# Storing half of the gate weights and all merge weights one superblock later, with x's root row by way of DRAM, cross-attention sums in one matmul, and a rank for readers of the dense banks

## The chip, the cores and the metric

The kernel runs on one core of one Trainium2 chip. The metric is the device time of one execution in microseconds (us). Before the change the median of three runs is 2143.12 us (2143.11 to 2143.8).

In the profile PE is the matmul engine and PEld its weight loads, DVE the vector engine, ACT the scalar engine, POOL GpSimd, and SP the queue that issues most DMAs.

## The reference

One decoder layer over x (2048 tokens x 1024, float32). `h = RMSNorm(x)` is multiplied by one wide matrix `w_in`; its columns feed three branches and their gates.

```
h = rms_norm(x, norm_g);  p = h @ w_in            # 59 blocks of 128 columns
y_a = rwkv7_mix(...)   * silu(z_a)                # delta-rule recurrence, 8 heads x 64
y_b = sliding_window_sink_attn(...) * silu(z_b)   # window 128, 8 query heads x 64
y_c = memory_cross_attn(q, mem ...) * silu(z_c)   # 4 heads x 128, 256 memory tokens
gates = sigmoid(p_gate)                           # 3 x 1024 columns
merged = gates0*(y_a @ w_proj_a) + gates1*(y_b @ w_proj_b) + gates2*(y_c @ w_proj_c)
out = x + merged @ w_out
```

In the cross attention each query head is divided by the root of its mean square over 128 channels; h divides x by such a root over 1024 channels.

## The kernel before

The 2048 tokens are worked off in four superblocks (`sb` 0 to 3) of 512 tokens. Activations lie with channels on the partitions, 512 tokens along a row.

**Dense products.** Float32 accuracy comes from three matmuls in a reduced format (float32r): every operand is split into a high part and the rest, and `gemm3` issues high x high (L534), high x low (L535) and low x high (L536). `proj` (one column block of `w_in`) is 8 such triples into one of two PSUM banks named `mm`; `gate` is a `proj` followed by a tanh on ACT (L1302), `merge` adds 4 triples with a block of `w_proj` and takes the product up on DVE (L1314 or L1317). The 24 column blocks from `B_G` on are those of the gates. `output` multiplies the merged rows by `w_out` (L1334 to L1336). `shift` reads an `mm` bank three times: ACT L739, DVE L740 and, last, DVE L742 (`carry`).

**Weights.** `wblock` fetches half a column block: a raw block of 256 KB (L514) is split by ACT (L515) and DVE (L516) into `whl`, 512 KB. One of the uses also stores the split pair to DRAM (L520), and later uses only load the pair (L511). `keep_at(key)` says at which use a block is stored: 0 for nearly all, 1 for odd blocks of `w_out` and for odd output blocks of branch 0's merge. A block is used once in each superblock. `whl` has 7 buffers, `raw` 3.

**Two streams and a planner.** In a superblock `stream_r` (the recurrence: `rwkv_prep`, `rwkv_inverse`, `rwkv_chain`) and `stream_f` (`cross_head`, `swa_kv`, four `swa_pair` beside the merge of branch 2, the merge of branch 1, the gates of branch 0) are woven together, and `x_sums` adds up the squares of the next superblock's x beside them. The order written that way only gives ranks: `steps` and `lay_out` play the whole program through with assumed durations, on each engine take the ready instruction of lowest rank, and fix that order on PE, DVE, ACT, POOL and SP. Splits and loads of weights get a rank 1000 lower, and an instruction that is not PE's and reads a PSUM bank gets 600 lower.

**The places that the change touches.** `cross_head` sums q*q over the partitions with `spread_sums`: ACT copies the square's high part (L557), DVE makes the rest (L558), and two matmuls with a matrix of ones add them up (L559, L560); this is so in superblocks 1 to 3. `x_scales` turns the sums of `x_sums` into roots on POOL (`rpow`), and `bcast_T` spreads them: a DVE copy (L572), four PE transposes (L574), an ACT copy (L1371) into `rb`. `x_cols` multiplies the next x by `rb` (L1383) and splits it into `hH` and `hL`. `rwkv_chain` fetches its operands chunk by chunk (`big<-fq`, L941, and `big<-fb`, L944); `put` (L758) has stored them.

Of the kernel before, what the change touches and what calls it, by code (L numbers as in the profile page):

```python
# [9 lines left out]
F32 = mybir.dt.float32  # L10
# [5 lines left out]
ALU = mybir.AluOpType  # L16
# [131 lines left out]
def steps(instructions, manual, groups, follow, ahead=1000):  # L148

    out, masks, seen, byname, opener = [], {}, {}, {}, {}  # L150
    for ins in instructions:
        if isinstance(ins, mybir.BassTilePoolBoundary):
            continue
        s = Step(ins, masks)
        for rs, w in ((s.reads, False), (s.writes, True)):
            for name, parts, words, _, psum, _ in rs:
                s.before |= {q for q, w2, p2, m2 in seen.get(name, ()) if (w or w2 or psum) and q is not s and p2 & parts and m2 & words}
        for name, parts, words, *_ in s.reads:
            seen.setdefault(name, []).append((s, False, parts, words))
        for name, parts, words, *_ in s.writes:  # L160
            old = seen.setdefault(name, [])
            old[:] = [x for x in old if x[0] is s or x[2] & ~parts or x[3] & ~words] + [(s, True, parts, words)]
        s.before |= {byname[x] for x in manual.get(ins.name, ())}
        s.before |= {opener.setdefault(r[0], s) for r in s.writes + s.reads} - {s}
        for b in s.before:
            b.after.append(s)
        byname[ins.name] = s
        s.rank = len(out)
        if any(r[0].startswith(("whl", "raw")) and (s.bytes or r[5] == F32R) for r in s.writes):
            s.rank = max(s.rank - ahead, min(s.rank, FRONT))  # L170
        if s.eng != "PE" and any(r[4] for r in s.reads):
            s.rank -= 600
        if s.eng == "DVE" and s.writes and s.writes[0][0].startswith(("ibc", "Yi")):
            s.rank += 500
        out.append(s)
    for a, b in follow.items():
        byname[a].next = byname[b]
    for names in groups:
        group = [byname[n] for n in names]
        group[0].group = group[1:]  # L180
        needs = set().union(*(s.before for s in group)) - set(group)
        for s in group:
            for b in needs - s.before:
                b.after.append(s)
            s.before |= needs
    return out
# [132 lines left out]
def build(tc, A, nsb=4):  # L319
# [19 lines left out]
    def g2(dt=F32, shape=(128, TB)):  # L339
        return gp_.tile(list(shape), dt, name="g2")  # L340
# [155 lines left out]

    def keep_at(key):

        return key[2] % 2 if key[0] == "out" or key[:2] == ("proj", 0) else 0

    def two_parts(raw):

# [52 lines left out]
    def spread_sums(out, w, sq, hi, lo):  # L555

        S.activation(hi, sq, AF.Copy)  # L557
        V.tensor_tensor(lo, sq, hi.bitcast(F32), op=ALU.subtract)  # L558
        PE.matmul(out, w, hi, start=True, stop=False)  # L559
        PE.matmul(out, w, lo, start=False, stop=True)  # L560
# [509 lines left out]
    def cross_head(h, sb, hT, yh, yl):  # L1070
        kv = rp.tile([128, 4, M], F32R, name="km", bufs=2)
        km = kv[:, :2]
        nc.sync.dma_start(km.bitcast(F32), Kd[h // 2][:, :, h % 2])
        if sb:
            vm = kv[:, 2:].rearrange("p u (k c) -> p u k c", k=2)
            nc.sync.dma_start(vm.bitcast(F32), Vs[:, :, :, h * 128:(h + 1) * 128])
        else:
            vm = kv[:, 2].bitcast(F32).rearrange("p (k c) -> p k c", k=2)
            nc.sync.dma_start(vm, Vd[:, :, h * 128:(h + 1) * 128])
        o = proj(B_XQ + h, hT)  # L1080
        qh, ql = g2(F32R), g2(F32R)
        S.activation(qh, o, AF.Copy)
        V.tensor_tensor(ql, o, qh.bitcast(F32), op=ALU.subtract)
        sq = g2()
        S.activation(sq, o, AF.Square)
        yield 1.717
        st = s_ps()
        rs = xp.tile([128, 8], F32, name="st8", bufs=2)
        if sb >= FIRST:
            spread_sums(st, onesw, sq, *(g2(F32R), g2(F32R)))  # L1090
            for i in range(4):
                tk = slice(i * 128, (i + 1) * 128)
                V.tensor_tensor_reduce(sq[:, tk], st[:, tk], ident, 1.0, 0.0, ALU.mult, ALU.add, rs[:, i:i + 1])  # L1093
        else:
            tok_stat(sq, 1, 4, st)
            V.tensor_copy(rs[:, :4], st[:, :4])
        rpow(rs[:, :4], rs[:, :4], 128 * EPS)
        mx = xp.tile([128, 8], F32, name="mx", bufs=2)
        sps = []
        for t2 in range(2):  # L1100
            sp = s_ps().rearrange("p (a m) -> p a m", a=2)
            for i in range(2):
                tk = slice((2 * t2 + i) * 128, (2 * t2 + i + 1) * 128)
                gemm3(sp[:, i], [((qh[:, tk], ql[:, tk]), (km[:, 0], km[:, 1]))])
            V.tensor_reduce(mx[:, 2 * t2:2 * t2 + 2], sp, axis=AX.X, op=ALU.max)
            sps.append(sp)
        V.scalar_tensor_tensor(mx[:, :4], mx[:, :4], -1.0, rs[:, :4], op0=ALU.mult, op1=ALU.mult)
        prs = []
        for t2 in range(2):
            pr = g2(shape=(128, 2, M))  # L1110
            for i in range(2):
                q = 2 * t2 + i
                S.activation(pr[:, i], sps[t2][:, i], AF.Exp, scale=rs[:, q:q + 1], bias=mx[:, q:q + 1],
                             accum_out=mx[:, 4 + q:5 + q])
            prs.append(pr)
        dn = xp.tile([128, 8], F32, name="dn", bufs=2)
        V.tensor_scalar(dn[:, :4], mx[:, 4:], 2.0, None, op0=ALU.mult)
        V.reciprocal(dn[:, :4], dn[:, :4])
        yield 5.667
        if not sb:  # L1120
            oo = o_ps()
            for t2 in range(2):
                pt = s_ps().rearrange("p (k i t) -> p k i t", k=2, i=2)
                for i in range(2):
                    q = 2 * t2 + i
                    scaled_by(prs[t2][:, i], dn[:, q:q + 1], sb)
                    for kt in range(2):
                        PE.transpose(pt[:, kt, i], prs[t2][:, i, kt * 128:(kt + 1) * 128], ident)
                pts = g2(shape=(128, 2, 256))
                S.activation(pts.rearrange("p k t -> p (k t)"), pt.rearrange("p k i t -> p (k i t)"), AF.Copy)  # L1130
                for kt in range(2):
                    PE.matmul(oo[:, t2 * 256:(t2 + 1) * 256], vm[:, kt], pts[:, kt], start=kt == 0, stop=kt == 1)
        else:
            for q in range(4):
                scaled_by(prs[q // 2][:, q % 2], dn[:, q:q + 1], sb)
            pts = []
            for kt in range(2):
                pt = s_ps()
                for q in range(4):
                    PE.transpose(pt[:, q * 128:(q + 1) * 128], prs[q // 2][:, q % 2, kt * 128:(kt + 1) * 128], ident)  # L1140
                pts.append((g2(F32R), g2(F32R)))
                S.activation(pts[kt][0], pt, AF.Copy)
                V.tensor_tensor(pts[kt][1], pt, pts[kt][0].bitcast(F32), op=ALU.subtract)
            oo = o_ps()
            gemm3(oo, [((vm[:, 0, kt], vm[:, 1, kt]), pts[kt]) for kt in range(2)])
        yield 3
        z = silu2(B_ZC + h, hT, gp_.tile([128, TB], F32, name="gt", bufs=2))
        V.tensor_tensor(z, oo, z, op=ALU.mult)
        split_y(z, yh, yl, "c", h, sb)
        yield 6.427  # L1150
# [209 lines left out]
    def x_scales(sb, ss=None):  # L1360

        if not sb:
            rs = row_sums(x0)
        else:
            rs = xp.tile([128, 4], F32, name="rs", bufs=2)
            V.tensor_tensor(rs, ss[:, :, 0], ss[:, :, 1], op=ALU.add)
        rpow(rs, rs, EPS, 1.0 / D)
        bc = s_ps()
        bcast_T(bc, rs, 1, 4)
        rb = tmp()  # L1370
        S.activation(rb, bc, AF.Copy)  # L1371
        return rb
# [23 lines left out]
    for sb in range(nsb):  # L1396
# [41 lines left out]
        gates = []  # L1438
        ss = xp.tile([128, 4, 2], F32, name="ss", bufs=2)
        streams = [paced(g, PACE[min(sb, 1)][i]) for i, g in enumerate((stream_r(), stream_f()))]  # L1440
        if sb + 1 < nsb:
            streams.append(x_sums(sb + 1, ss))
        for _ in weave(*streams):
            pass
        for p in range(4):
# [1 line left out]
        rb = None  # L1447
        if sb + 1 < nsb:
            rope_tables(sb + 1)
            rb = x_scales(sb + 1, ss)  # L1450
        parts = []
        for o in range(8):
            for _ in merge(0, *ya, accs, hT, gates=gates, orange=(o,)):
# [96 lines left out]
```

## Time and profile before

| | |
|---|---|
| profiled execution, its own time | 2143.2 us |
| its span | 2141.4 us |
| TensorE clock granted | 1.0 |
| PE busy | 2125.9 us, 14260 instructions |
| DVE busy | 1418.5 us |
| ACT busy | 802.1 us |
| DMA engines, superblock 0 (540 us) | mostly 0.7 to 1.0 of their time |
| dense triples L534, L535, L536 on `hH`/`hL` | 1888 of each |
| weight stores `k<-whl` | 162 of 512 KB |
| weight reloads `whl<-k` | 474 of 512 KB |

A busy PE is counted from modelled ends: one 128x512 matmul is given some 390 ns, while the next one starts sooner. So the time that one takes from the stream is read from the starts of neighbours, not from its duration. The 1.8 us between the execution's time and the span lie outside of the instructions.

### The profile page before, as it was taken

Reading aid. Unit: us, or ns where it says so; the run is one execution under the profiler, and the core shown is the slowest. Engines: PE = TensorE matmul, PEld = TensorE weight load, DVE = VectorE, ACT = ScalarE, POOL = GpSimd, SP = SyncE. Lnnn points to the kernel's source line nnn. Section 1 sums busy time; section 2 is a strip of 40 time slices with the busy share of each in tenths; the row PEclk is TensorE's granted clock in tenths of the full one; section 3 lists DMA queues with packets and bytes.
Section 4 is the critical chain, followed back from the end, with each engine's and each line's share of the span. In section 5 each row is a group of like instructions: output and inputs, shape, how many; then the busy total and the mean of one; then the engine's idle time right before and its main releaser. Section 6 shows DMA issues by size and latency. Waiting matters only on the chain.

```text
span 2141.4 us, 37426 instructions
## 1 busy us (share of the span) xinstructions
PE 2125.9 (99%) x14260; PEld 1753.8 (82%) x14260; DVE 1418.5 (66%) x3234; ACT 802.1 (37%) x1699; POOL 133.6 (6%) x180
## 2 busy tenths in 40 slices
PE   9999999999999999999999999999999999999999
PEld 7888887778888888878888888887888888888787
DVE  7879888468576787546647778736455777873532
ACT  7655554326344353303424434420423334331220
POOL 1001000001001000001000000000100010000000
PEclk9999999999999999999999999999999999999999
DMA  9988888987866678695876667777676676768665
GB/s 331 364 282 271 272 289 283 340 294 251 285 203 205 192 218 239 198 311 193 281 254 211 201 180 228 236 231 260 216 264 220 197 204 199 233 186 269 217 206 181
DMA packets 308594, 519.17 MB, mean 242 GB/s; under 512 B 89280, under 2 KB 175552, under 8 KB 308416
## 3 DMA queue, kind: packets, MB, share of 16 engines
q1 hardware_dynamic: 292288, 487.42, 70.9%
q10 hardware_dynamic: 16128, 29.37, 4.2%
q8 instruction: 113, 1.85, 0.4%
q14 instruction: 65, 0.53, 0.1%
HBM read 378.80 MB, written 137.89 MB: 241 GB/s over the span
## 4 chain that ended last, share of the span: by engine, by line
PE 91%; DVE 4%; DMA 3%; ACT 1%; issue 1%; POOL 0%; SPq 0%; ACTq 0%; DVEq 0%; POOLq 0%
PE mm L534 23%; PE mm L535 23%; PE mm L536 23%; PE mm L1334 1%; PE mm L1336 1%; PE mm L1335 1%; DMA raw<-in_w_in 1%; PE rw L1016 1%; PE rw L999 1%; PE oo L1283 1%; DVE whl L516 1%; PE rw L831 1%; PE rw L850 1%; DMA k<-whl 1%; PE oo L831 1%
## 5 line engine op out<-in xcount | busy, mean ns | idle before, releaser
L534 PE MATMUL mm<-hH,whl 128*128 128x512 f32 x1888 | 745.2, 395 | 2.0 <-DVE carry L742 1.4
L535 PE MATMUL mm<-hL,whl 128*128 128x512 f32 x1888 | 743.5, 394 | 0.0
L536 PE MATMUL mm<-hH,whl 128*128 128x512 f32 x1888 | 742.5, 393 | 0.0
L534 PEld LDWEIGHTS mm<-hH,whl 128*128 128x128 f32 x1888 | 354.8, 188 | 74.4 <-ACT whl L515 1.8
L536 PEld LDWEIGHTS mm<-hH,whl 128*128 128x128 f32 x1888 | 354.7, 188 | 71.4
L535 PEld LDWEIGHTS mm<-hL,whl 128*128 128x128 f32 x1888 | 355.0, 188 | 70.1 <-DVE hL L1386 0.2
L515 ACT ACTIVATE whl<-raw 128x512 fp32r<-128x512 f32 x174 | 109.1, 630 | 186.4 <-PE mm L536 131.7
L516 DVE TENSOR_TENSOR whl<-raw,whl 128x512 fp32r<-128x512 f32 x174 | 119.2, 687 | 61.7 <-ACT whl L515 55.7
L534 PE MATMUL mm<-yh,whl 128*128 128x512 f32 x384 | 151.4, 394 | 1.3 <-DVE gt L1317 1.2
L535 PE MATMUL mm<-yl,whl 128*128 128x512 f32 x384 | 150.3, 391 | 0.0
L536 PE MATMUL mm<-yh,whl 128*128 128x512 f32 x384 | 149.7, 390 | 0.0
L1302 ACT ACTIVATE gt<-mm 128x512 f32<-128x512 f32 x64 | 37.8, 590 | 179.3 <-PE mm L536 179.0
L534 PEld LDWEIGHTS mm<-yh,whl 128*128 128x128 f32 x384 | 72.1, 188 | 17.2 <-DVE gt L1317 1.6
L1317 DVE SCALAR_TENSOR_TENSOR gt<-gt,mm 128x512 f32<-128x512 f32 x32 | 21.9, 686 | 95.5 <-PE mm L536 95.3
L535 PEld LDWEIGHTS mm<-yl,whl 128*128 128x128 f32 x384 | 72.1, 188 | 15.0 <-DVE yl L1065 0.5
L536 PEld LDWEIGHTS mm<-yh,whl 128*128 128x128 f32 x384 | 72.1, 188 | 14.7
L487 POOL TENSOR_SCALAR st<-st 128x4 f32<-128x4 f32 (+1 forms) x32 | 12.7, 397 | 1019.7 <-DVE st L1093 418.8
L1341 DVE SCALAR_TENSOR_TENSOR ya<-mm,ya 128x512 f32<-128x512 f32 x16 | 11.0, 689 | 93.8 <-PE mm L1336 93.8
L1251 ACT ACTIVATE g<-g,mxs,st 128x128 f32<-128x128 f32 x128 | 61.6, 484 | 28.1 <-DVE mxs L1244 28.1
L892 DVE TENSOR_TENSOR ibc<-km,Yi 128x126 f32<-128x126 f32 (+22 forms) x248 | 62.9, 254 | 7.7 <-DMA km<-fn 2.1
L893 DVE TENSOR_TENSOR Yi<-Yi,ibc 128x126 f32<-128x126 f32 (+22 forms) x248 | 62.7, 253 | 5.6
L491 POOL TENSOR_TENSOR st<-st,mhalf 128x8 f32<-128x8 f32 (+1 forms) x36 | 52.7, 1463 | 3.0
(1828 smaller groups left out, 3579.5 us busy)
## 6 DMA issues: line engine op xcount, KB each, us to landing
whl<-k SPq DMA_DIRECT2D x474, 512.0 KB, 4.2
k<-whl SPq DMA_DIRECT2D x162, 512.0 KB, 4.8
raw<-in_w_in SPq DMA_DIRECT2D x118, 256.0 KB, 4.2
fq<-big SPq DMA_DIRECT2D x64, 256.0 KB, 4.4
fb<-big SPq DMA_DIRECT2D x64, 256.0 KB, 4.3
big<-fq SPq DMA_DIRECT2D x32, 512.0 KB, 6.4
big<-fb SPq DMA_DIRECT2D x32, 512.0 KB, 5.6
ya<-in_x ACTq DMA_DIRECT2D x32, 256.0 KB, 4.7
```

What stands on the lines that cost most here:

```text
L491: G.tensor_tensor(out, out, mhalf[:, :n], op=ALU.pow)
L515: S.activation(w[:, 0], raw, AF.Copy)
L516: V.tensor_tensor(w[:, 1], raw, w[:, 0].bitcast(F32), op=ALU.subtract)
L534: PE.matmul(out, lh, rh, start=i == 0, stop=False)
L535: PE.matmul(out, lh, rl, start=False, stop=False)
L536: newest[0] = PE.matmul(out, ll, rh, start=False, stop=i == n - 1).ins.name
L831: m = PE.matmul(g[:, c], BK[h, c0 + c], Q[h, c0 + c], start=True, stop=True)
L892: V.tensor_tensor(bc[:, :m, :w], Nb[:, s, s + 1:].unsqueeze(1).to_broadcast([128, m, w]), B[:, :m, s:s + 1].to_broadcast([128, m, w]), op= ...
L893: V.tensor_tensor(B[:, :m, s + 1:], B[:, :m, s + 1:], bc[:, :m, :w], op=ALU.add)
L1251: S.activation(P_, P_, AF.Exp, scale=r2[:, b, i:i + 1], bias=mx[:, b, i:i + 1], accum_out=mx[:, b, 2 + i:3 + i])
L1302: S.activation(t, gp, AF.Tanh, scale=0.5)
L1317: V.scalar_tensor_tensor(g, g, 1.0, pp, op0=ALU.add, op1=ALU.mult)
```

## The change

- `keep_at` now also says 1 for odd halves of the gates' column blocks (24) and odd output blocks of the merges of branches 1 and 2 (8): these 32 half blocks are stored in superblock 1 instead of 0, and so are fetched raw and split there once more.
- In `cross_head`, superblocks 1 to 3, DVE first adds the lower 64 rows of the squares to the upper 64; the high part (ACT) and the rest (DVE) of the 64 sums lie one below the other in one tile, and one matmul adds up all 128 rows.
- `x_scales` now runs as a part of the third stream, behind `x_sums`; for superblocks 1 to 3 its roots are stored as a row of 512 numbers in DRAM, and one DMA loads that row into all 128 partitions of `rb`.
- Readers of an `mm` bank get a rank 1600 lower instead of 600.

```diff
         if s.eng != "PE" and any(r[4] for r in s.reads):
-            s.rank -= 600
+            s.rank -= 600 + 1000 * any(r[0].startswith("mm_") for r in s.reads)
...
     def keep_at(key):
-        return key[2] % 2 if key[0] == "out" or key[:2] == ("proj", 0) else 0
+        return key[2] % 2 if key[0] in ("out", "proj") or key[0] == "in" and key[1] >= B_G else 0
...
         if sb >= FIRST:
-            spread_sums(st, onesw, sq, *(g2(F32R), g2(F32R)))
+            half = g2(F32R)
+            V.tensor_tensor(sq[EV], sq[EV], sq[OD], op=ALU.add)
+            S.activation(half[EV], sq[EV], AF.Copy)
+            V.tensor_tensor(half[OD], sq[EV], half[EV].bitcast(F32), op=ALU.subtract)
+            PE.matmul(st, onesw, half, start=True, stop=True)
...
         rpow(rs, rs, EPS, 1.0 / D)
+        if sb:
+            row = dp.tile([1, TB], F32, name=f"xr{sb}")
+            nc.sync.dma_start(row[0].rearrange("(i t) -> t i", t=128), rs)
+            return row
         bc = s_ps()
         bcast_T(bc, rs, 1, 4)
...
+        rows = []
+
+        def stream_x():
+            yield from x_sums(sb + 1, ss)
+            rows.append(x_scales(sb + 1, ss))
+
         if sb + 1 < nsb:
-            streams.append(x_sums(sb + 1, ss))
+            streams.append(stream_x())
...
             rope_tables(sb + 1)
-            rb = x_scales(sb + 1, ss)
+            rb = tmp()
+            nc.sync.dma_start(rb, rows[0].to_broadcast([128, TB]))
```

Since the planner runs anew, the order moves on every engine. Three places in superblock 0 follow. In the changed kernel the lines behind L1087 stand 4 further down (L1275 is the old L1271, L1306 the old L1302), those behind L1371 by 8, and the numbers in tile names differ.

DVE, at the fourth `rwkv_prep`: `mm_3002` is the bank with that head pair's k, `rw`, `oo` and `yps` are banks with its small products, `as_` banks of the window attention. Before:

```order
L839 TENSOR_TENSOR big_2203<-oo_2653,gmask_179 64x512
L839 TENSOR_TENSOR big_2202<-yps_2652,gmask_179 64x512
L516 TENSOR_TENSOR whl_3320<-raw_3321,whl_3320 128x512
L740 SCALAR_TENSOR_TENSOR rk__3041<-mm_3002,c_pv_105,rk__3041 128x511
L1271 TENSOR_TENSOR g2_3121<-as__3114,over_181 64x256
L742 COPY carry1_215<-mm_3002 128x1
```

The same place on DVE in the changed kernel, where the bank is `mm_2990`:

```order
L839 TENSOR_TENSOR big_2202<-yps_2646,gmask_179 64x512
L516 TENSOR_TENSOR whl_3308<-raw_3309,whl_3308 128x512
L1275 TENSOR_TENSOR g2_3109<-as__3102,over_181 64x256
L1275 TENSOR_TENSOR g2_3121<-as__3114,over_181 64x256
L821 SCALAR_TENSOR_TENSOR rr__2521<-rr__2521,dv_182,rk__2245 128x512
L516 TENSOR_TENSOR whl_3450<-raw_3451,whl_3450 128x512
L846 TENSOR_TENSOR big_2205<-big_2205,Pl_658 128x1024
L740 SCALAR_TENSOR_TENSOR rk__3029<-mm_2990,c_pv_105,rk__3029 128x511
L1297 TENSOR_TENSOR g2_3228<-yps_3125,g2_3228 128x512
L742 COPY carry1_215<-mm_2990 128x1
```

Between the last product of the small banks and the last reader of the dense bank (L742) stand eight instructions now instead of three: L821, which lets the next k have its buffer, has moved behind them. On PE the banded product (L1283, now L1287) and eight transposes (L850) have moved in front of the dense block that takes over this bank.

SP, just before `rwkv_chain` begins: `fb` and `fq` are the stored operands of the chain. Before:

```order
L758 DMA fb0_1_654<-big_3000 128x4x128
L514 DMA raw_5350<-in_w_in 128x512
L520 DMA k114_5223<-whl_5218 128x1024
L514 DMA raw_5397<-in_w_in 128x512
L520 DMA k115_5230<-whl_5225 128x1024
L944 DMA big_4254<-fb0_0_653 128x1024
L941 DMA big_4262<-fq0_0_651 128x1024
```

The same place on SP in the changed kernel:

```order
L758 DMA fb0_1_654<-big_2988 128x4x128
L514 DMA raw_5347<-in_w_in 128x512
L514 DMA raw_5354<-in_w_in 128x512
L944 DMA big_4230<-fb0_0_653 128x1024
L941 DMA big_4238<-fq0_0_651 128x1024
```

The two weight stores between the last `put` and the chain's first fetch of `fb` are gone.

ACT, in the merge of branch 2 beside the last window pair: `gt` is a gate's buffer, `mm_4519` (`mm_4491`) the bank of its product. Before:

```order
L515 ACTIVATE whl_4782<-raw_4783 128x512
L1064 ACTIVATE yh_4249<-g2_4101 128x512
L515 ACTIVATE whl_4790<-raw_4791 128x512
L515 ACTIVATE whl_4797<-raw_4798 128x512
L1302 ACTIVATE gt_4558<-mm_4519 128x512
```

The same place on ACT in the changed kernel:

```order
L515 ACTIVATE whl_4750<-raw_4751 128x512
L1296 ACTIVATE g2_4221<-oo_4104 128x512
L1064 ACTIVATE yh_4225<-g2_4077 128x512
L1306 ACTIVATE gt_4528<-mm_4491 128x512
L515 ACTIVATE whl_4756<-raw_4757 128x512
```

The gate's tanh, which reads the dense bank, has moved in front of two splits of weights.

## The prediction

> **What bounds the kernel.** I read the page first: span, busy time by engine, and the chain that ended last.
>
> ```profile
> span 2141.4 us, 37426 instructions
> PE 2125.9 (99%) x14260; PEld 1753.8 (82%) x14260; DVE 1418.5 (66%) x3234; ACT 802.1 (37%) x1699; POOL 133.6 (6%) x180
> PE 91%; DVE 4%; DMA 3%; ACT 1%; issue 1%; POOL 0%; SPq 0%; ACTq 0%; DVEq 0%; POOLq 0%
> ```
>
> PE is both the busiest engine and nine tenths of the chain. So a gain can come from two things only: work taken out of PE's stream, and PE's waits. The busy time by stretches tells where there are any:
>
> ```profile
> core 0: us, PE busy (x) PEld busy (x) DVE busy (x) ACT busy (x) POOL busy (x), PEclk, DMA share, GB/s
> 100.00:540.00 440.00, 433.43 (x3072) 355.27 (x3071) 341.40 (x751) 218.57 (x452) 32.56 (x41) 1.00 0.86 286
> 540.00:1050.00 510.00, 510.00 (x3462) 421.19 (x3461) 333.04 (x775) 178.64 (x381) 31.42 (x41) 1.00 0.73 228
> 1600.00:2100.00 500.00, 500.00 (x3417) 412.97 (x3416) 307.12 (x728) 156.57 (x342) 26.05 (x31) 1.00 0.69 216
> ```
>
> From 540 us on PE never stands still. Nearly all that can be won back lies in superblock 0, where 6.6 of 440 us are idle; DVE is at 0.78 there and the DMA engines at 0.86. What PE waits for, longest total first (who waits, for whom: us, times, longest):
>
> ```profile
> PE oo L383 <- ACT onesw L380: 2.4, 1, 2.4
> PE rw L1008 <- DMA big<-fb: 1.6, 1, 1.6
> PE mm L534 <- DVE carry L742: 1.4, 1, 1.4
> PE mm L534 <- DVE gt L1317: 1.2, 1, 1.2
> PE rw L1016 <- DVE Zt L1014: 0.9, 1, 0.9
> ...
> PE as__3964 L1232 <- DVE g L1238: 0.6, 1, 0.6
> ```
>
> The first is the start of the program, which the change leaves alone. The other five, 5.7 us together, are single events in superblock 0, and a new order deals them anew.
>
> **Work taken out of PE.** In the twelve cross heads of superblocks 1 to 3 two matmuls become one, so twelve 128x512 matmuls go. What one costs is read from the starts of the first and the last of 21 in an unbroken run:
>
> ```profile
> 575.29 0.39 PE L534 MATMUL mm<-hH,whl 128*128 128x512 f32 x1
> ...
> 579.83 0.39 PE L536 MATMUL mm<-hH,whl 128*128 128x512 f32 x1
> ```
>
> 4.54 us for 20 steps is 0.227 us, and twelve are 2.7 us. The four transposes of x's roots go three times; here is the second set in its place:
>
> ```profile
> 1044.15 0.39 PE L535 MATMUL mm<-yl,whl 128*128 128x512 f32 x1
> 1044.38 0.60 PE L574 MATMUL as__11187<-c_ident,rt 128*128 128x128 f32 x4
> 1044.74 0.48 PE L536 MATMUL mm<-yh,whl 128*128 128x512 f32 x1
> 1045.05 0.40 PE L534 MATMUL mm<-yh,whl 128*128 128x512 f32 x1
> ```
>
> From L535 to L534 are 0.90 us; without the transposes two steps would be 0.45. Three times 0.45 is 1.4 us. Both stand in a saturated stream, so I count them whole: -4.1 us. The orders show no other change in what PE executes.
>
> **The chain's first fetch (SP).** Here are SP's issues before the wait for `big<-fb`, the wait, and that stretch by engines:
>
> ```profile
> 405.20 2.15 SPq L520 DMA_DIRECT2D k<-whl  x1
> ...
> 407.46 0.37 SPq L944 DMA_DIRECT2D big<-fb  x1
> ...
> 414.27 0.46 PE L1008 MATMUL rw<-W,big 64*64 64x64 f32 x16 [1.58 <-DMA big<-fb]
> ```
>
> ```profile
> 400.00:420.00 20.00, 18.42 (x165) 14.63 (x163) 8.95 (x18) 4.42 (x8) 0.00 (x0) 1.00 0.97 330
> ```
>
> The DMA engines are full (0.97), and SP needs 2.15 us to issue one store, with the fetch queued behind it. In the changed order the two stores ahead of that fetch are gone, and with them 1 MB: at the row's 330 GB/s some 3.2 us of transfers. That is more than the 1.6 us of the wait; the 0.9 us wait for `Zt` 8 us later belongs to the same late chain. I count both, -2.5 us (bounds: 0, if the fetch is waited for elsewhere, and -2.5).
>
> **Readers of the dense banks first (ACT, DVE).** ACT before the wait for L1317, which stands at 361.2 us:
>
> ```profile
> 359.62 1.15 ACT L515 ACTIVATE whl<-raw 128x512 fp32r<-128x512 f32 x2 [1.10 <-PE mm L536]
> ...
> 360.67 0.58 ACT L1302 ACTIVATE gt<-mm 128x512 f32<-128x512 f32 x1
> ```
>
> Both `mm` banks are full there: one waits for L1317 on DVE, one for this L1302. In the changed order the tanh stands ahead of the two splits, 1.15 us sooner, and PE's next dense block can take its bank: nearly the whole 1.2 us. The 0.6 us for L1238 are less sure (copies of the window attention keep their rank); together I count -1.4 us, bounds 0 and -1.8.
>
> **A bank that is freed later (DVE).** The same rank does not help where the reader itself is not ready. At the fourth key block the bank is freed by L742:
>
> ```profile
> 262.38 0.69 DVE L516 TENSOR_TENSOR whl<-raw,whl 128x512 fp32r<-128x512 f32 x1
> ...
> 263.10 0.75 DVE L740 SCALAR_TENSOR_TENSOR rk__3041<-mm,c_pv,rk__3041 128x511 f32<-128x511 f32 x1
> 263.77 0.41 DVE L1271 TENSOR_TENSOR g<-as__3114,over 64x256 f32<-64x256 f32 x1
> ...
> 264.10 0.14 DVE L742 COPY carry<-mm 128x1 f32<-128x1 f32 x1
> 264.38 0.47 PE L534 MATMUL mm<-hH,whl 128*128 128x512 f32 x1 [1.36 <-DVE carry L742]
> ...
> 266.00 1.23 DVE L846 TENSOR_TENSOR big<-big,Pl 128x1024 f32<-128x1024 f32 x1
> ```
>
> Behind the small banks' last product DVE needed 0.69 + 0.75 + 0.41 + 0.14 = 2.0 us up to L742. Now it is 0.69 + 2 x 0.41 + 0.69 + 0.69 + 1.23 + 0.75 + 0.69 + 0.14 = 5.7 us (L821 and L1297 taken at 0.69 like L516, all 128x512 on DVE): 3.7 us later. PE has other work ahead of that block now, the banded product and eight transposes:
>
> ```profile
> 266.38 0.32 PE L1283 MATMUL oo<-g,Vt 64*64 64x128 f32 x1
> ...
> 268.61 0.48 PE L536 MATMUL mm<-hH,whl 128*128 128x512 f32 x1
> ```
>
> That covers 2.2 us, and the wait grows by 1.5 us, to 2.9 (bounds 0 and 3.7).
>
> **The 32 weight blocks.** In superblock 0 they save 32 stores of 512 KB; in superblock 1 they cost the same stores, but raw loads half as large, and 32 more splits on ACT and DVE (last column: idle before):
>
> ```profile
> L515 ACT ACTIVATE whl<-raw 128x512 fp32r<-128x512 f32 x174 | 109.1, 630 | 186.4 <-PE mm L536 131.7
> L516 DVE TENSOR_TENSOR whl<-raw,whl 128x512 fp32r<-128x512 f32 x174 | 119.2, 687 | 61.7 <-ACT whl L515 55.7
> ```
>
> ```profile
> 780.00:820.00 40.00, 40.00 (x280) 33.33 (x277) 35.57 (x64) 14.51 (x26) 0.00 (x0) 1.00 0.74 217
> ```
>
> 32 x 0.63 = 20 us of ACT and 32 x 0.69 = 22 us of DVE go beside 510 us of PE in which DVE has 177 us left. The cover is thin at 780:820 alone, with 4.4 us of DVE free in 40. Superblock 0 is the nearest picture of a DVE so full, and it loses 5.7 us in 440 by its waits. Twelve of the splits (8 of branch 2's gates and 4 of its merges) stand beside the window pairs; some 60 us of that are as full, and 60 x 5.7 / 440 is +0.8 us (bounds 0 and 8.2, twelve splits with no cover).
>
> **The new order elsewhere.** It may set waits that I cannot see: +0.9 us, a sixth of the 5.7 (bounds 0 and 5.7). The cross sums' chain gets one DVE step of 64x512 more, 0.7 us at most, with PE's other work planned into it. No cost.
>
> **x's roots through DRAM.** The price of a scattered row store isn't in the trace. The nearest row is the 1 KB load of `bones`, 4.9 us to landing; behind it the copy that ends the way of before, and the use:
>
> ```profile
> c_bones<-in_bones SPq DMA_DIRECT2D x1, 1.0 KB, 4.9
> ```
>
> ```profile
> 525.44 0.58 ACT L1371 ACTIVATE rt<-as__5914 128x512 f32<-128x512 f32 x1
> ```
>
> ```profile
> L1383 DVE TENSOR_TENSOR rt<-rt x8: 681/682/685, 537.8 to 549.0; 128x512 f32<-128x512 f32 x8
> ```
>
> Two such DMAs are 9.8 us instead of DVE, PE and ACT. `rb` is done at 526.0 now, is used at 537.8, and PE takes the next h at 575.3: 26 us between the last L1383 and that. SP stands until the row has landed, with loads of `w_out` behind it, at 2.7 us of PE each (12 x 0.227). Six of seven `whl` buffers are 16 us of lead, less 5.5 for load and split: a row that lands within 10.5 us costs nothing. *What a page says against it:* the Trainium skill, "DMA: Bandwidth & Descriptors", section "Rules for kernel authors", has a strided last dim become one descriptor per element, 512 here; with its 10.5 ns a packet and 2.0 us fixed (sections "Bandwidth" and "Anatomy of one DMA") my estimate would be 7.4 us. That page measured both on GpSimd's queue, and no run here shows them yet. By it the sum stays as it is, but only 3 us of the lead are left, and I would give the rival below 0.05 where the rows give it 0.02. The order also has two more table loads on ACT at the end of superblock 1, each like this one:
>
> ```profile
> 523.61 1.28 ACT L612 ACT_TABLE_LOAD   x1
> ```
>
> 2.6 us on an ACT that is idle for over half of that superblock (178.64 busy of 510): nothing.
>
> **Sum**, against the profiled execution's 2143.2 us (median 2143.12, so the same): -4.1 -2.5 -1.4 +1.5 +0.8 +0.9 = -4.8, that is 2138.4 us.
>
> **Rivals.** "No change" here means within 0.2%, 4.3 us, about what a measurement of this kernel can tell.
>
> - *The waits of superblock 0 are only dealt anew*, and come to what they were: what stays is PE's work, 2143.2 - 4.1 = 2139.1, and with 0.8 from superblock 1 2139.9. For it: five single events of 0.6 to 1.6 us, one of which I find grown. Against it: the chain's fetch has a cause that the change removes.
> - *DVE falls behind in superblock 1* (slower). Place: the window pairs, 740 to 860 us. Split halves come late, and the dense blocks wait one by one. Price: 8.2 us if none of twelve splits finds a gap, 22 if none of 32. My gain without the two guesses is 6.5 us, so from 6.5 + 4.3 = 10.8 us of waits on it decides; at 12 us the time is 2143.2 - 6.5 + 12 = 2148.7. Against it: the stretches around hold 7 to 16 us of idle DVE.
> - *The row store holds SP* (slower): beyond 10.5 us to landing each further us costs 3, once a superblock; at 20 us 28 us, 2167. No DMA of the trace takes that long.
>
> **How the numbers follow.** My sum 0.54 (2134.5 to 2138.8), dealt anew 0.39 (2138.8 to 2143), DVE behind 0.05, row store 0.02. The first two carry the range: 2134.0 (sum with its two guesses at 0, -6.5, and most of the remaining waits gone) to 2143.0. Faster by over 0.2%: 0.54; within: 0.39; slower: 0.07.
>
> **What would show it.** 36 matmuls on the sums' lines (12 new, 24 old) instead of 48 for cross heads and window pairs, and no L574 after 50 us but the key's. No wait of L1008 for `big<-fb` and a shorter DMA share from 380 to 460 us; the L1302 wait at 361 us gone; a PE wait of nearly 3 us for L742 near 264 us. PE without idle from 540 us on, but for less than 1 us from 700 to 880. A row landing in under 10 us. I am wrong if superblock 0's idle does not fall under its 6.6 us, or if a DVE wait of several us appears in superblock 1.

## The result, and the profile after

| | before | after |
|---|---|---|
| median | 2143.46 us (2143.11 to 2143.92) | 2166.76 us (2163.81 to 2170.24) |
| ratio | | 1.0109, 95% interval 1.0097 to 1.0121 |
| profiled execution, its span | 2143.2, 2141.4 us | 2167.6, 2165.8 us |

The changed kernel is 23 us slower. Its page (span, busy time, chain by engine):

```profile
span 2165.8 us, 37520 instructions
PE 2128.5 (98%) x14236; PEld 1751.6 (81%) x14236; DVE 1447.7 (67%) x3275; ACT 822.8 (38%) x1730; POOL 141.9 (7%) x180
PE 85%; DVE 6%; DMA 6%; issue 1%; ACT 1%; POOL 1%; SPq 0%; ACTq 0%; DVEq 0%; POOLq 0%
```

PE has 24 instructions fewer (12 matmuls and 12 transposes), as the edits say, and its share of the chain falls from 91% to 85%. What PE waits for now, in total, times, longest:

```profile
PE mm L1338 <- ACT whl L515: 10.6, 1, 10.6
PE mm L534 <- DVE g L1321: 7.2, 2, 6.8
PE mm L1338 <- DVE g L1321: 4.0, 2, 3.3
PE oo L383 <- ACT onesw L380: 2.4, 1, 2.4
PE oo L1287 <- DVE g L1275: 1.0, 1, 1.0
```

The first three are new, and one event makes most of each. Where they lie, by busy time in stretches; first four stretches of before:

```profile
100.00:500.00 400.00, 393.43 (x2893) 322.66 (x2892) 304.73 (x686) 195.75 (x413) 28.83 (x38) 1.00 0.87 290
500.00:560.00 60.00, 60.00 (x268) 49.19 (x268) 52.67 (x91) 31.39 (x52) 3.73 (x4) 1.00 0.79 258
1040.00:1090.00 50.00, 50.00 (x225) 41.36 (x224) 29.07 (x47) 13.92 (x22) 1.81 (x3) 1.00 0.88 304
1560.00:1610.00 50.00, 50.00 (x224) 41.40 (x223) 24.57 (x40) 9.68 (x15) 1.77 (x3) 1.00 0.81 273
```

and the same view of after (length; PE, PEld, DVE, ACT and POOL busy; granted clock; DMA share; GB/s):

```profile
100.00:500.00 400.00, 396.03 (x2915) 326.39 (x2914) 307.48 (x689) 200.81 (x421) 29.80 (x38) 1.00 0.77 251
500.00:560.00 60.00, 55.86 (x236) 44.65 (x235) 49.67 (x85) 27.16 (x45) 4.51 (x3) 0.97 0.79 234
600.00:1040.00 440.00, 438.69 (x3137) 360.19 (x3137) 315.00 (x741) 172.72 (x374) 31.36 (x38) 1.00 0.76 238
1040.00:1090.00 50.00, 39.39 (x168) 32.17 (x167) 30.33 (x50) 14.61 (x25) 1.77 (x3) 0.90 0.80 231
1560.00:1610.00 50.00, 41.76 (x175) 33.52 (x174) 25.60 (x42) 13.67 (x22) 1.78 (x3) 0.93 0.71 207
```

Superblock 0 lost 6.6 us of 400 before and 4.0 now. The ends of superblocks 0, 1 and 2, where PE stood for nothing before, lose 4.1, 10.6 and 8.2 us. The row of x's roots is stored at just these three places. SP's queue at the second (start, duration of the issue, what):

```profile
1046.98 0.37 SPq L1374 DMA_DIRECT2D xr<-rs  x1
1050.68 0.33 SPq L514 DMA_DIRECT2D raw<-in_w_out  x1
1058.02 0.32 SPq L1465 DMA_DIRECT2D rt<-xr  x1
...
1067.70 0.33 SPq L514 DMA_DIRECT2D raw<-in_w_out  x1
```

The load of the row is issued 11.0 us after the store. The whole kernel's DMA list has the row, 2 KB, beside blocks of 256 KB (times, KB each, median us to landing):

```profile
raw<-in_w_out SPq DMA_DIRECT2D x24, 256.0 KB, 3.2
rt<-xr SPq DMA_DIRECT2D x3, 256.0 KB, 5.6
xr<-rs SPq DMA_DIRECT2D x3, 2.0 KB, 11.0
```

SP's own waits say how long it stood for that:

```profile
SPq L1465 <- DMA xr<-rs: 25.0, 3, 9.5
```

But that is not all. The raw block issued at 1050.68, ahead of SP's wait, was late too; here its line alone, from 1048 to 1066 us:

```profile
L514 SPq DMA_DIRECT2D raw<-in_w_out x1: 333/333/333, 1050.7 to 1050.7; - x1
...
DMA to landing us min/median/max: 12.0/12.0/12.0
```

12.0 us where the median is 3.2. All transfers crawl while the row drains, as 3-us stretches of after show (last three numbers: clock, DMA share, GB/s):

```profile
1047.00:1050.00 3.00, 3.00 (x15) 2.49 (x14) 2.30 (x5) 1.15 (x2) 0.52 (x1) 1.00 1.02 375
...
1053.00:1056.00 3.00, 3.00 (x15) 2.49 (x14) 0.00 (x0) 0.00 (x0) 0.00 (x0) 1.00 0.68 40
1056.00:1059.00 3.00, 0.56 (x3) 0.14 (x1) 0.00 (x0) 0.00 (x0) 0.00 (x0) 1.00 0.37 70
1059.00:1062.00 3.00, 0.00 (x0) 0.00 (x0) 0.00 (x0) 0.00 (x0) 0.00 (x0) 0.70 0.85 160
1062.00:1065.00 3.00, 0.00 (x0) 0.00 (x0) 1.21 (x2) 0.63 (x1) 0.00 (x0) 0.50 0.95 347
```

The stretch from 1053 to 1056 in the kernel before:

```profile
1053.00:1056.00 3.00, 3.00 (x15) 2.46 (x14) 3.00 (x5) 1.14 (x2) 0.00 (x0) 1.00 1.06 392
```

So 40 GB/s with several large transfers under way, where it was 392. Not only SP's transfers are late: three loads of x's columns that ACT issued on its own queue from 1048.5 to 1049.4 us landed after 9.6 to 11.6 us, where the median before is 4.8. ACT and DVE do nothing from 1053 on, PE from 1056.6. ACT's timeline at the end of superblock 2 shows its part:

```profile
1579.32 11.46 ACTq L1388 DMA_DIRECT2D rt<-in_xt  x5
1590.83 0.63 ACT L1326 ACTIVATE g<-mB 128x512 fp32r<-128x512 f32 x1 [10.88 <-DMA rt<-in_xt]
```

Five issues of x's column loads, 0.4 us each, took ACT 11.46 us, and the gates' step L1326 stood behind them. The last of them ran at 1590.42, as the row had landed at 1590.40; the two share no data, so that the one waits for the other is read from the times only. At the end of superblock 1 ACT's last such issue came at 1062.7 us, as the raw block issued at 1050.68 had landed.

### The profile page after: what moved, and what is told of

Read it like the earlier page. It is cut to its first block, busy times and chain, and to the rows that moved or that the text cites. A ratio compares the mean times of both kernels' runs of the same rounds, so it can differ in the third digit from the quotient of the medians.

```text
span 2165.8 us, 37520 instructions
## 1 busy us (share of the span) xinstructions
PE 2128.5 (98%) x14236; PEld 1751.6 (81%) x14236; DVE 1447.7 (67%) x3275; ACT 822.8 (38%) x1730; POOL 141.9 (7%) x180
## 4 chain that ended last, share of the span: by engine, by line
PE 85%; DVE 6%; DMA 6%; issue 1%; ACT 1%; POOL 1%; SPq 0%; ACTq 0%; DVEq 0%; POOLq 0%
PE mm L534 21%; PE mm L535 21%; PE mm L536 21%; PE mm L1338 1%; DVE whl L516 1%; PE mm L1340 1%; PE mm L1339 1%; DMA xr<-rs 1%; DMA rt<-in_positions 1%; PE rw L1016 1%; PE rw L999 1%; DMA raw<-in_w_out 1%; PE rw L831 1%; PE oo L1287 1%; PE rw L850 1%
## 5 line engine op out<-in xcount | busy, mean ns | idle before, releaser
L516 DVE TENSOR_TENSOR whl<-raw,whl 128x512 fp32r<-128x512 f32 x206 | 141.9, 690 | 80.3 <-ACT whl L515 78.6
L515 ACT ACTIVATE whl<-raw 128x512 fp32r<-128x512 f32 x206 | 129.0, 627 | 156.4 <-PE mm L536 104.7
L1306 ACT ACTIVATE gt<-mm 128x512 f32<-128x512 f32 x64 | 38.0, 594 | 196.3 <-PE mm L536 196.3
L1345 DVE SCALAR_TENSOR_TENSOR ya<-mm,ya 128x512 f32<-128x512 f32 x16 | 11.0, 689 | 92.2 <-PE mm L1340 92.2
L1321 DVE SCALAR_TENSOR_TENSOR gt<-gt,mm 128x512 f32<-128x512 f32 x32 | 22.0, 687 | 75.5 <-PE mm L536 68.6
L1338 PE MATMUL mm<-whl,g 128*128 128x512 f32 x128 | 50.9, 397 | 15.8 <-ACT whl L515 10.6
```

The lines of the kernel that those rows point to most:

```text
L515: S.activation(w[:, 0], raw, AF.Copy)
L516: V.tensor_tensor(w[:, 1], raw, w[:, 0].bitcast(F32), op=ALU.subtract)
L1306: S.activation(t, gp, AF.Tanh, scale=0.5)
L1321: V.scalar_tensor_tensor(g, g, 1.0, pp, op0=ALU.add, op1=ALU.mult)
L1338: PE.matmul(op[tt], mh[k][:, tk], wh, start=k == 0, stop=False)
```

## The experiments

All ratios are against the kernel before on the same chip (its median there 2142.6 to 2144.1 us), with 95% intervals.

**Is it the row?** The row taken out of the changed kernel, and put alone into the kernel before.

```
 e1   - nc.sync.dma_start(row..., rs) / dma_start(rb, row.to_broadcast)
      + bcast_T(bc, rs, 1, 4); S.activation(rb, bc, AF.Copy)
 e2   the row alone, the other parts as before
```

> The changed kernel with one part taken back: x's roots are spread again by four transposes after the rope tables, and no row goes to DRAM. Theory (the row is the cause: its 512 four-byte elements, 11.0 us to landing, hold transfers and queues at the ends of superblocks 0 to 2): the three PE stalls of 3.4, 10.8 and 7.0 us and the half-clock stretches behind them go, and the rest of the change stays: 2137 to 2141 us, faster than before. Rival (the new order of readers and the blocks kept later make the ends of superblocks late, the row only lies beside them): the stalls stay, 2158 us or more.

> The kernel before with the row through DRAM as its only edit. Theory (row): stalls at the three superblock ends as in the changed kernel, 2160 to 2172 us. Rival (order of readers and kept blocks): 2141 to 2144 us, no stall above 1 us at the superblock ends.

Measured: e1 2142.62 us, 0.9997 (0.9988 to 1.0007); e2 2170.91 us, 1.0128 (1.0111 to 1.0145). The row is the loss, 24 us in the changed kernel (1.0109 less 0.9997) and 27 alone. e1 came out above its 2141: the rest of the change gave less than I reckoned (below).

**SP's stand, or the pieces?** The same store, with nobody to read it; then that store with a quarter of the pieces, in the same order; then twice.

```
 e4   store as in the changed kernel; rb from bcast_T, no load of the row
 e16  e4 with row.rearrange("(t i) -> t i", i=4)      # 128 pieces of 16 bytes
 e6   e4 with a second store, to a row of its own     # 1024 pieces of 4 bytes
```

> The changed kernel with the scattered store kept where it is, but read by nobody: the roots in use are spread by the four transposes as before. If only SP's stand between the store and the load that needs it costs time: 2137 to 2142 us, as with the row undone. If the 512 pieces themselves hold the DMA engines, so that loads issued beside them land 6 to 9 us late and ACT's loads wait for the row's landing: stalls of several us stay, 2148 to 2165 us.

> The kernel whose row nobody reads, with the row stored as 128 pieces of 16 bytes instead of 512 of 4; the order of instructions is the same, and no load waits for the store. Between the row undone (none: -0.9 us against the kernel before) and 512 pieces (+15.3 us), if the loss goes by pieces: 1 to 6 us above the kernel before, with the store landing 4 to 5 us after issue. Rival (any store at this place deals the transfers and ACT's loads anew and costs the same): 2155 to 2160 us.

> The kernel whose scattered row nobody reads, with the same row stored a second time right behind it, read by nobody too: 1024 pieces instead of 512 at each of three superblock ends. Theory (the price goes by pieces, which pass the DMA engines one behind the other): the second store lands about 20 us after its issue, and the loss against the row undone grows from 16 us to 35 to 50: 2177 to 2192 us. Rival (a store costs a fixed time to land, or the loss comes from one wait that is there anyway): 2157 to 2165 us.

Measured: e4 2158.78 us, 1.0073 (1.0058 to 1.0088); e16 2142.11 us, 0.9997 (0.9988 to 1.0006); e6 2166.45 us, 1.0106 (1.0091 to 1.0121). So 16 of the 24 us come with nobody reading the row, and with 5.0 us of waits of SP put down to its landing (one, ahead of a load that does not need it) instead of 25.0. PE's waits and the store's landing in e4:

```profile
PE mm L1338 <- ACT hH L1397: 5.8, 1, 5.8
PE mm L1338 <- DVE g L1321: 4.5, 2, 4.0
PE mm L1338 <- ACT whl L515: 2.5, 1, 2.5
```

```profile
xr<-rs SPq DMA_DIRECT2D x3, 2.0 KB, 10.8
```

and in e16:

```profile
PE mm L1338 <- DVE g L1321: 0.9, 2, 0.5
```

```profile
xr<-rs SPq DMA_DIRECT2D x3, 2.0 KB, 2.9
```

The same 2 KB at the same place cost 16 us in 512 pieces and nothing in 128, less than the 1 to 6 us that I expected of e16. e6 missed its 2177 to 2192: the two stores landed after 8.5 to 11.7 us, side by side, not one behind the other, and the second cost 7 us, not 16 or more. The loss is no fixed price per piece. The number of the pieces, their size and where they lie in DRAM change together in e16, so which of the three decides stays open; the store on another queue was not tried either.

**The other 8 us.** The load of the row put later on SP; then 16-byte pieces in the changed kernel, without and with the later load; then one transpose ahead of the store.

```
 e5   + self.late = ... 12000 if any(r[0].startswith("xr") for r in self.writes) else 0
 e3   row.rearrange("(t i) -> t i", i=4); DVE reads rb.rearrange("p (t i) -> p i t", i=4)
 e7b  e3 with self.late = ... 6000
 e8   + PE.transpose(rT[:4, :128], rs, ident); V.tensor_copy(r4, rT[:4, :128])
      row stored from r4: 4 pieces of 512 bytes
```

> The changed kernel, with the planner told that the row's store lands 12 us later than it reckons: the load that reads the row is put three to five weight transfers later on SP, the rest of the order is nearly the same. Theory (two causes: SP stands for the row, worth the 8 us between the changed kernel and the one whose row nobody reads, and the 512 pieces hold up transfers and ACT's loads, worth the other 16): SP's 25 us of waiting for the row all but go, the stalls stay, 2154 to 2162 us. Rival (SP's stand costs nothing, what costs 8 us is that the columns of x wait for the row's way out and back): 2163 to 2170 us.

> The changed kernel, but the row lies in DRAM by token within a tile first, so that the store is 128 pieces of 16 bytes and not 512 of 4; DVE reads the loaded row with a stride of four. The order of instructions is the changed kernel's own. Theory with the price by piece: landing falls from 11.0 us to 4 to 6 us, SP's wait for it falls from 8 us to about 3, the stalls all but go, 2137 to 2145 us. Rival (the price is that of any store that has to be read back from DRAM, or of what waits in the order): 2155 us or more, with SP still standing 8 us.

> The 16-byte version of the row, with the planner told that its store lands 6 us later than it reckons, so that the load is put later on SP. Theory (what was left of the loss with 16-byte pieces, 9.5 us over the row undone, is SP's stand for the row and transfers put behind it): 2142 to 2149 us. Rival (it is the 128 pieces and ACT's stands): 2150 to 2155 us.

> The changed kernel, but one transpose on PE turns the 128 x 4 roots into 4 rows of 128 before the store, which then is 4 pieces of 512 bytes. With 512 pieces landing after 11.0 us and 128 after 4.1 to 4.7, a straight line gives 17 ns a piece and about 2 us for none: theory (the pieces are the price) expects landing 2 to 3 us and 2140 to 2147 us. Rival (what is left with few pieces is the way out to DRAM and back, with the load's 5 us and the transfers dealt anew): 2148 to 2153 us, as with 16-byte pieces.

Measured: e5 2159.74 us, 1.0072 (1.0048 to 1.0096), with no wait of SP for the row's landing left: without that stand the kernel is 8 us faster (1.0109 less 1.0072, with some 6 us either way by the two intervals). The time is that of e4, but the waits are not: PE waits 4.8 us for L1321 and, in the output's product, 6.3 us for L1345, which e4 does not have.

e3 2152.16 us, 1.0043 (1.0028 to 1.0058), SP's wait 5.6 us in all; e7b 2148.60 us, 1.0030 (1.0017 to 1.0042); e8 2149.61 us, 1.0029 (1.0020 to 1.0038). e7b met its range, e3 missed its 2145, and e8 missed its 2147 and came out in its rival's range. How long e8's store took to land its trace does not say. Few pieces make the stalls near the store shorter (e3 still has waits of 3.0 and 3.4 us) or take them away (e7b, e8), but with every row that goes out and back at the superblock's end 7 us or more over the row undone are left. Most of that in e7b and e8, and a part of it in e5, is a wait in the output's product, in e8 some 23 us behind the load's issue:

```profile
PE mm L1338 <- DVE ya L1345: 4.3, 2, 2.4
```

**ACT's stand.** The loads of x's columns on GpSimd's queue, PE's order the same.

```
 e7a  - nc.scalar.dma_start(xt, A["xt"]...)   + nc.gpsimd.dma_start(xt, A["xt"]...)
```

> The changed kernel with the loads of x's columns (in_xt) issued on GpSimd's queue instead of ScalarE's; PE's order is the same. Theory (ACT stands 9 to 14 us at each superblock end, because its fourth or fifth load of x has to wait until the row or a transfer beside it has landed, and the gates' steps on ACT stand behind it): ACT's long stands go, 2148 to 2160 us. Rival (the blocks of w_out and the kept blocks land late themselves, ACT's stand lies beside that): 2162 to 2170 us.

Measured: 2173.27 us, 1.0141 (1.0126 to 1.0156): a miss, slower still. ACT's long stands were gone, and DVE stood in their place, behind the row's load:

```profile
DVE rt L1391 <- DMA rt<-xr: 18.4, 2, 10.9
```

So ACT's stand lies beside a second lateness of the same length; taking away one of them gains nothing. The comparison is not a clean one: on GpSimd's queue the column loads landed after 10.3 us (median), on ACT's after 6.1.

**The place.** The sums of x asked for earlier, so that the same 512 pieces drain in the middle of the superblock; then with 128 pieces; then without the kept blocks.

```
 e12  - yield 45   + yield 25          # in x_sums
 e13  e12 with e3's row
 e17  e12 with keep_at as before
```

> The changed kernel with x's sums of squares asked for every 25 us of the plan instead of every 45: the row, still 512 pieces of 4 bytes, is stored some 120 transfers of SP earlier, in the middle of the superblock, and read back where it was read before. Theory A (the price hangs on the place: at the superblock's end the load is two transfers behind the store, and PE, ACT and DVE live from hand to mouth there): SP's wait for the row goes, transfers beside the store still land 10 us and more after issue, but PE hardly waits there; 2139 to 2147 us. Rival B (wherever the pieces drain, weights land later than PE's stock of them lasts): stalls of several us move to the middle of superblocks 0 to 2, 2150 to 2160 us.

> The same early row with 128 pieces of 16 bytes. Theory A: as the run before, 2138 to 2146 us, since neither SP's wait nor PE's stalls are left to save. Rival B: 4 to 10 us less than the run before, since fewer pieces hold the weights for a shorter time. If x's columns still come late because of the load's own 5 us (what few pieces left at the superblock's end, 6 to 9 us), both early kernels stay 4 us or more above the row undone.

> The early scattered row (stored in the middle of the superblock) without the kept blocks: the best two pieces of what was seen so far, the kernel without row and kept blocks (ratio 0.9991) and a row that costs nothing at its place but saves 12 transposes (3 x 4 at 0.112 us, 1.4 us). If both hold, 2 to 4 us below the kernel before, which beats both kernels; if x's columns come late because of the way out and back, 1 us below to 2 us above it.

Measured: e12 2145.61 us, 1.0011 (1.0002 to 1.0020); e13 2149.08 us, 1.0033 (1.0023 to 1.0043); e17 2145.07 us, 1.0012 (1.0003 to 1.0021). Theory A holds for e12. Transfers beside the store are slow at the new places too: the raw block issued behind the first row, at 333.7 us, landed after 7.8 us, and a 512-KB pair behind the third after 12.4. PE does not wait in the 20 us around any of the three:

```profile
336.00:339.00 3.00, 3.00 (x17) 2.59 (x16) 2.97 (x8) 2.61 (x7) 0.00 (x0) 1.00 0.42 44
339.00:342.00 3.00, 3.00 (x17) 2.53 (x15) 3.00 (x8) 1.05 (x3) 0.00 (x0) 1.00 0.52 44
```

The 44 GB/s alone would prove little, since less is asked for there; in e1 the same two stretches have 111 and 182. The 3 us between e12 and e1 lie elsewhere: PE's idle from 100 to 500 us is 7.0 us in e12 and 3.9 in e1, and the wait of L1008 for `big<-fb` is back with 1.8.

e13 is slower than e12, with fewer pieces. Its reads of the row with a stride explain a part; the product of x and row in e13:

```profile
L1393 DVE TENSOR_TENSOR rt<-rt x24: 1056/1074/1103, 535.7 to 1573.8; 128x512 f32<-128x512 f32 x24
```

and in e12:

```profile
L1391 DVE TENSOR_TENSOR rt<-rt x24: 678/682/693, 536.9 to 1570.0; 128x512 f32<-128x512 f32 x24
```

8 x 0.39 us a superblock, between row and columns; e3 and e7b pay it too. That such columns are what PE waits for in the output's product is argued from these runs, not shown alone. e17 promised 2 to 4 us and gave none.

**The other parts,** without the row: each left out of e1, and each alone in the kernel before.

```
 e9   e1 with s.rank -= 600          e14  before with the new rank only
 e10  e1 with keep_at as before      e15  before with the new keep_at only
                                     e11  before with the halved sums only
```

> The row undone and the earlier rank of dense banks' readers undone too: halved cross sums and kept blocks are left. By the prediction's terms (12 matmuls -2.7 us, the chain's first fetch -2.5, splits +0.8, new order +0.9): 3.5 us below the kernel before, about 2140 us; the bank's wait at 264 us and the waits of about 2 us at 1052 to 1055 us, seen with the row undone, go. Rival (the new waits come from the kept blocks): they stay, 2142 to 2144 us.

> The row undone and the kept blocks undone: halved cross sums and the readers' rank are left. By the prediction's terms (-2.7 for the matmuls, -1.4 for the readers, +1.5 for the bank): 2.6 us below the kernel before, about 2141 us, with the chain's first fetch waiting again at 414 and 422 us (1.6 and 1.0 us). Rival (the new order costs what the matmuls save): 2142 to 2144 us.

> The kernel before with the halved cross sums alone. By the prediction's term (12 matmuls at 0.227 us): 2.7 us below the kernel before, about 2141 us, waits as before. Rival (the matmuls taken out lie where PE waits for DVE or ACT anyway, or the three steps of DVE and ACT that replace them make PE wait): within 1 us of the kernel before.

> The kernel before with the earlier rank of dense banks' readers alone. By the prediction's terms: readers -1.4 us (361 us), bank +1.5 us (264 us), in all within 1 us of the kernel before. Rival (the rank is what gives the kernel without row and kept blocks its 1.9 us): 2 to 4 us below it.

> The kernel before with the later keeping of half the blocks alone. By the prediction's terms: first fetch -2.5 us (waits at 414 and 422 us gone), splits +0.8, order +0.9: 0.8 us below the kernel before. Rival (32 more splits on ACT and DVE in superblock 1 make PE wait there): 1 us or more above it, with new waits between 520 and 1060 us.

Measured: e9 2143.08 us, 0.9999 (0.9990 to 1.0008); e10 2141.35 us, 0.9991 (0.9982 to 1.0000); e11 2145.27 us, 1.0008 (0.9999 to 1.0017); e14 2144.95 us, 1.0008 (0.9999 to 1.0017); e15 2142.89 us, 1.0003 (0.9994 to 1.0012). None of the five can be told from the kernel before with certainty. e10 met its 2141, e9 came out in its rival's range, and e11, e14 and e15 in neither of their two. e10 is the best kernel seen, 1.9 us below the kernel before by its ratio, with an interval that ends at no change. In e10 (whose profiled execution was the slowest of its eleven) the chain's first fetch is waited for again:

```profile
PE rw L1008 <- DMA big<-fb: 2.3, 1, 2.3
```

while in e15, with the kept blocks alone, the same wait is down to

```profile
PE rw L1008 <- DMA big<-fb: 0.5, 1, 0.5
```

But this wait does not go by the kept blocks. Without them it is 0.4 us in e14 and in no list of e2, e11 and e17; with them it is 0.8 in e9 and 1.8 in e12. In e11 two weight stores still stand on SP between the last `put` and the fetch, as before, and PE does not wait.

And e11, where twelve matmuls less should have shown, has 2.5 us of waits that the kernel before does not have:

```profile
PE rw L850 <- DVE big L846: 2.5, 3, 0.8
```

## Why the prediction was wrong, step by step

- **x's roots through DRAM, taken at 0: the step that failed.** It let the row cost only SP's stand, and gave that 10.5 us of cover. The row landed after 11.0 us, 0.5 past the cover; by the prediction's own 3 us for each us beyond, 1.5 us. It cost 24. Shown in its place: the 512 pieces cost 16 us with nobody reading the row, by what they do to the transfers beside them, and 128 pieces of the same bytes nothing (e4, e16). Having the row read costs the other 8, and they go when the load is put later (e5). The two do not simply add up, for with few pieces and no stand of SP 7 us are left (e7b, e8), and why is argued, not shown.

  The cover was reckoned for weights that land in 5.5 us with their split; the raw block issued beside the row took 12.0 us to land alone. Nor did PE have 16 us of work in hand: it stopped 9.6 us after the store's issue at the second end, for weights, and 10.4 and 7.7 us after it at the first and third, for the gates' products. And ACT, whose column loads I never put on the row's path, stood 11 us with those products' steps behind it. I had taken the price from `c_bones`, a load of about as many bytes (1 KB); the pieces, not the bytes, made the time: 2.9 us for 128 of them, 10.8 for 512.
- **The rule that I had weighed against it.** By the Trainium skill, "DMA: Bandwidth & Descriptors", "Rules for kernel authors", a strided last dim is one descriptor an element; the fall from 10.8 to 2.9 us with a quarter of the pieces agrees. My estimate of 7.4 us from its figures was 3.4 us short, and nothing in it said that other transfers would crawl.
- **The rival "the row store holds SP"** had its time right (2167) and its place, at 0.02; its mechanism makes up about a third of the loss, and its condition, a landing of 20 us, was not met. That the time agrees is luck.
- **Superblock 0: right as a sum, in part by luck.** -2.5 for the first fetch, -1.4 for the readers and +1.5 for the bank are -2.4; PE's idle from 100 to 500 us fell by 2.6, from 6.6 to 4.0. But it is 3.3 in e2, which has the row alone, and 4.6 in e11, whose halved sums begin in superblock 1; in e12 and e17 it is 7.0 and 6.8. So much of it is the rival "dealt anew". The fetch's waits went in the changed kernel, but that the two stores had caused them is not shown: they went in e11 with both stores in place. The rank's terms are better borne out. With the rank alone (e14) the wait for L1317 is gone, and the bank's wait came in another form: 0.4 us for L742, 1.0 for L1275's banded product and 1.0 for L846's transposes, where I saw 2.9 for L742. Without the rank (e9, e11, e15) L742 keeps its 1.4.
- **PE's work, -4.1: the count was right** (24 instructions), but work taken out shows only where nothing takes its place. With the row undone the transposes are back, and -2.7 for the matmuls is left; the halved sums alone measured 1.7 us above the kernel before, with an interval from no change to 3.6. Its idle from 500 to 2100 us is 5.7 us, where it was 0. What the 12 transposes are worth was not measured alone.
- **New order elsewhere and splits, +1.7: too small.** With the row undone PE's idle in 500 to 560, 600 to 1040, 1040 to 1090, 1100 to 1560 and 1610 to 2100 us is 0.9, 0.8, 1.5, 1.1 and 0.2, together 4.4 where it was 0; in the five kernels with other parts left out (e9 to e11, e14, e15) it is 1.8 to 5.7 from 500 us on. A new order brings such waits whichever part brings the new order. So my sum without the row (-3.4) became -0.9: matmuls -2.7, superblock 0 -2.6, new waits +4.4. The medians differ by just that, but the profiled execution of e1 took 1.0 us more than that of before, so 1.9 us of this account stay open. "DVE falls behind in superblock 1" did not happen; from 540 to 1040 us PE waits for DVE no longer than 0.5 us at a time.

## What to carry to other kernels

Before a small store goes into a full stream of transfers, count its pieces, not its bytes, and ask what else is in flight while they drain and which engine has issues of its own behind them: a queue's cover is worth nothing if the cover's own transfers are slowed by the same store. If the pieces can't be made few, move the store to where every engine has stock; with the same 512 pieces the kernel lost 24 us at the superblock's end and some 3 with the store in its middle. And take the price of a DMA from a row of the same shape or leave it open wide: a nearest row that agrees in bytes alone is no bound. Where an edit makes a planner lay out the whole order anew, a wait that goes is not yet explained by the edit: look whether it goes in other new orders too.

## What the runs showed of the hardware

- A store of 512 four-byte pieces took 8.1 to 12.1 us to land, 128 pieces of 16 bytes 2.8 to 6.4 us, and two stores of 512 at once 8.5 to 11.7 us each. While 512 pieces drained at a superblock's end the core moved as little as 40 GB/s in the stretches above, with 256-KB blocks under way on two queues, and such blocks landed after 9.6 to 12.0 us.
- A long wait of PE is followed by half clock. In the rows above PE stands from 1056.6 us; a mean clock of 0.70 from 1059 to 1062 puts the step to half at some 1060.2, 3.6 us later. PE starts again so (start, duration):

```profile
1067.17 0.76 PE L1338 MATMUL mm<-whl,g 128*128 128x512 f32 x1 [10.61 <-ACT whl L515]
...
1069.01 0.63 PE L1339 MATMUL as__11509<-whl,g 128*128 128x512 f32 x1
1069.44 0.63 PE L1340 MATMUL as__11509<-whl,mB 128*128 128x512 f32 x1
...
1070.60 0.40 PE L1338 MATMUL mm<-whl,g 128*128 128x512 f32 x1
1070.83 0.40 PE L1339 MATMUL mm<-whl,g 128*128 128x512 f32 x1
```

  Steps of 0.43 us instead of 0.23 for 3.1 us. The wait of 6.8 us at the end of superblock 2 was followed by 3.1 us of such steps too; after the one of 3.3 us at the end of superblock 0 PE started at full clock, went to half 1.3 us later, and stayed there for 3.4 us. Seven or eight steps that are 0.2 us longer make some 1.5 us, an estimate of what each of the three costs beyond its length. The Trainium skill, "TensorE: Matmul & The Clock Gate", "Part 1: The HAM clock gate", has the clock halved after an idle window of about 3.4 us and full again after as long a busy one; the trace agrees, to a few tenths of a us.
- DVE's product of two 128x512 operands took 0.68 us, and 1.07 us with one of them read at a stride of four numbers (e12 and e13, above).
